# Chunked attention heads of a hybrid encoder layer: score products in two matmuls over stacked high and low halves instead of three

## The chip, the cores and the metric

The kernel runs on one core of one Trainium2 chip. The time is device microseconds (us) of one execution. Engines are named as the profile names them: PE is TensorE's matmul, PEld its weight load, DVE is VectorE, ACT is ScalarE, POOL is GpSimd, SP is SyncE, which here issues the DMAs.

## The reference

One layer: a mixer with eight heads of multi-head latent attention (MLA) and eight heads of chunked attention, then a gated MLP with a causal convolution. 1024 tokens, width 1024. What matters here is the chunked attention:

```python
CHUNK, LEFT_CHUNKS, CA_HEADS, CA_HEAD_DIM = 64, 8, 8, 64
BAND = (LEFT_CHUNKS + 1) * CHUNK

cq = rmsnorm(ca[:, :, 0], g_ca_q[l])
ck = rmsnorm(ca[:, :, 1], g_ca_k[l])
o_ca = chunk_attention(cq, ck, cv, rel_bias[l])

def one_chunk(args):                      # in chunk_attention
    qch, ci = args
    kb = lax.dynamic_slice_in_dim(k_pad, ci * CHUNK, BAND, axis=1)
    vb = lax.dynamic_slice_in_dim(v_pad, ci * CHUNK, BAND, axis=1)
    s = jnp.einsum('bqhd,bkhd->bhqk', qch, kb,
                   preferred_element_type=jnp.float32) * scale + bias[None]
    valid = kj >= (LEFT_CHUNKS - ci) * CHUNK
    s = jnp.where(valid[None, None, None, :], s, NEG_INF)
    p = jax.nn.softmax(s, axis=-1).astype(vb.dtype)
    return jnp.einsum('bhqk,bkhd->bqhd', p, vb)
```

All inputs are float32. The kernel's matmuls take a rounded format (`F32R`), so each float32 operand is split into a high part (the rounded value) and a low part (what is left), and a product is high by high plus high by low plus low by high.

## The kernel before

The attention part interleaves three kinds of work on PE. *Units* are attention: one unit is one head and one group of 512 query tokens, in four tiles of 128 queries. `scores` (line 633) makes a tile's scores, row minima, bias and exponentials, scales and splits the probabilities into 16-bit halves, and has them transposed by DMA; `values` (line 714) multiplies them by the values, three tiles later (`DEPTH`). After four tiles the output page of the unit goes out (lines 724 to 730), through a tile `sb` that ACT writes and DVE adds into a tile `o`, which SP stores. The 16 units of the chunked heads come first, in the order head pair `p`, group `g`, head `o` of the pair; then come 16 MLA units.

*Fillers* are projections: values 0, query-key 1 and 2, values 1, query-key 3, the latents (`f_m`), their up-projections and the output projection of the chunked heads. `pace` (line 810) lets a filler run for a multiple of the cost that `scores` and `values` return. In `gemm3_f` (line 158) each step of a filler is ordered behind the score or value group that stands `LAG` places before the newest one (the list `trail`). A filler of values loads its weights with `load_w` (line 170), whose squares (line 187) use the same two `sq` tiles as the norms of the query-key filler (line 368).

*Pages* are the operands of the scores. For a chunked pair (two heads, 512 tokens) `prep` in `ca_unit` builds a query page and a key page with `qk_page` (line 611): four transposes on PE into one PSUM bank (tag T, one buffer), ACT copies the high half (lines 618, 621), DVE subtracts for the low half (lines 619, 622). Rows 0 to 63 are the first head of the pair, rows 64 to 127 the second; the page's middle index is high or low. The query page has two buffers (tag Q), the key page three (tag K). MLA pages are built by the same function, with 96 rows.

In line 655 a tile's scores are, for each segment of up to 512 keys, query-high by key-high, query-high by key-low and query-low by key-high, over the head's 64 rows. Tiles 0 to 3 of a head have one segment of 128 to 512 keys, tiles 4 to 7 have two with 640 keys together.

The order of instructions on each engine is not written out by hand: the framework draws it from program order, from priorities (the offsets `OFF_S`, `OFF_P`, `OFF_V` pull scores, probabilities and values ahead) and from a simulated timeline. Each engine then works in order.

Of the kernel before, what the change touches and what calls it, by code (L numbers as in the profile page):

```python
# [23 lines left out]
P = 128  # L24
# [38 lines left out]
def layer_kernel(ctx, tc, I, out):  # L63
# [544 lines left out]
                sp.dma_start(part_d[t][:, n * 512:(n + 1) * 512], o[:])  # L608


    def qk_page(src, name, rows, tag, bufs, gain):

        pt = ps.tile([P, 512], F32, name=f"{name}_ps", tag="T", bufs=TB)
        for j in range(4):
            pe.transpose(pt[:rows, j * P:(j + 1) * P], src(j), ident[:])
        pg = at.tile([P, 2, 512], F32R, name=name, tag=tag, bufs=bufs)
        if gain is None:
            act.activation(pg[:rows, 0], pt[:rows], AF.Copy)
            dve.tensor_tensor(pg[:rows, 1], pt[:rows], f32(pg[:rows, 0]), op=SUB)
        else:  # L620
            act.activation(pg[:rows, 0], pt[:rows], AF.Copy, scale=gain)
            dve.scalar_tensor_tensor(pg[:rows, 1], pt[:rows], gain, f32(pg[:rows, 0]), op0=MUL, op1=SUB)
        return pg

    class Unit:

# [6 lines left out]
        def scores(u, i):  # L633

            qpg, kpgs = u.pages()
            bias = u.bias() if u.band else None
            lo = max(0, i - 4) if u.band else 0
            n = (i - lo + 1) * P
            nm = f"{u.nm}_{i}"
            rsum = cst.tile([P, 1], F32, name=f"rs{nm}", tag="rsum", bufs=4)  # L640
            ri = cst.tile([P, 1], F32, name=f"ri{nm}", tag="ri", bufs=4)
            with tc.high_priority(offset=OFF_S):
                s = ps.tile([P, 1024], F32, name=f"s{nm}", tag="S", bufs=2)
                n0 = max(0, min(4, i + 1) - lo) * P
                n1 = n - n0
                c0 = 512 - n0 if n1 else 0
                segs = [(c0, lo * P, n0, 0)] if n0 else []
                if n1:
                    segs.append((512, max(lo, 4) * P - 512, n1, 1))
                q = slice((i % 4) * P, (i % 4 + 1) * P)  # L650
                rs_ = slice(u.base, u.base + u.rows)
                for a in range(2):
                    for c, ko, w, kh in segs:
                        for b in range(2 - a):
                            last = pe.matmul(s[:, c:c + w], qpg[rs_, a, q], kpgs[kh][rs_, b, ko:ko + w],  # L655
                                             start=(a == 0 and b == 0), stop=(a == 1))
# [24 lines left out]
                act.activation(pr[:, :n], sv, AF.Exp, bias=m[:], scale=-1.0, accum_out=rsum[:, 0:1])  # L681
            with tc.high_priority(offset=OFF_P):
                dve.reciprocal(ri[:], rsum[:, 0:1])
                dve.tensor_scalar(ri[:], ri[:], PSCALE, None, op0=MUL)  # L684
                u.pt[i] = []
                for x, (p0, p1) in enumerate(pieces):
                    w = p1 - p0
                    cnt[0] += 1
                    spare = not u.band and cnt[0] % 2
                    if spare:  # L690
                        hl = apg.tile([P, 1024], F16, name=f"hl{nm}_{x}", tag="v16", bufs=6)
                    else:
                        hl = at.tile([P, 1280], F16, name=f"hl{nm}_{x}", tag="HL", bufs=HL_BUFS)
                    pp = pr[:, p0:p1]
                    mode = (MODE_C if u.band else MODE_M)[cnt[0] % 4]
                    if mode == "2":
                        scale_pool(pp, pp, ri[:])
                        act.activation(hl[:, :w], pp, AF.Copy)
                        pool.tensor_tensor(hl[:, w:2 * w], pp, hl[:, :w], op=SUB)
                    else:  # L700
                        if mode == "1":
                            scale_pool(hl[:, :w], pp, ri[:])
                        else:
                            act.activation(hl[:, :w], pp, AF.Copy, scale=ri[:])
                        dve.scalar_tensor_tensor(hl[:, w:2 * w], pp, ri[:], hl[:, :w], op0=MUL, op1=SUB)  # L705
                    if spare:
                        tt = apg.tile([P, 8, P], F16, name=f"PT{nm}_{x}", tag="v16", bufs=6)
                    else:
                        tt = at.tile([P, 10, P], F16, name=f"PT{nm}_{x}", tag="PT", bufs=PT_BUFS)
                    sp.dma_start_transpose(tt[:, :2 * w // P, :], hl[:, :2 * w])  # L710
                    u.pt[i].append((tt, lo + p0 // P, w // P))
            return sum(3 * max(107, w / 2.4) for _, _, w, _ in segs)

        def values(u, i):
            if i % 4 == 0:
                u.pv = ps.tile([P, 512], F32, name=f"pv{u.nm}_{u.g}", tag="pv", bufs=1)
            c = slice((i % 4) * P, (i % 4 + 1) * P)
            todo = [(lo + j, tt[:, h * nk + j, :]) for tt, lo, nk in u.pt[i] for j in range(nk) for h in range(2)]
            with tc.high_priority(offset=OFF_V):
                for x, (j, mov) in enumerate(todo):  # L720
                    last = pe.matmul(u.pv[:, c], u.vst(j), mov, start=(x == 0), stop=(x == len(todo) - 1))  # L721
                trail.append(last.ins)
                if i % 4 == 3:
                    sb = at.tile([P, 512], F32, name=f"sb{u.nm}_{u.g}", tag="sb", bufs=1)
                    dst = at.tile([P, 512], F32, name=f"o{u.nm}_{u.g}", tag="o", bufs=1)
                    r0, r1 = (slice(64, 128), slice(0, 64)) if u.odd else (slice(0, 64), slice(64, 128))
                    inv = vscale[u.vs][1]
                    act.activation(sb[r0], u.pv[r1], AF.Copy, scale=inv[r1])
                    dve.scalar_tensor_tensor(dst[r0], u.pv[r0], inv[r0], sb[r0], op0=MUL, op1=ADD)
                    sp.dma_start(u.dst_d[r0, u.g * 512:(u.g + 1) * 512], dst[r0])  # L730
            return 56 * len(todo)

# [12 lines left out]
    def ca_unit(p, g, o):  # L745
        def prep():
            if g == 0:
                load_bias(2 * p + o)
            if o == 0:
                q = qk_page(lambda j: qns[p, g][:, j, 0:128], f"q{p}_{g}", P, "Q", 2, None)  # L750
                k = qk_page(lambda j: qns[p, g][:, j, 128:256], f"k{p}_{g}", P, "K", 3, gk_ca[:])
                pages["c", p, g] = (q, k)
        u = Unit(f"c{p}{o}", 64 * o, 64,
                 lambda: (pages["c", p, g][0], [pages["c", p, i][1] for i in range(g + 1)]),
                 lambda j: vts[p, j // 4][:, j % 4, o].rearrange("p a b -> p (a b)"),
                 g, True, lambda: biases[2 * p + o], o, oT_d[4 + p], ("c", p // 2))
# [602 lines left out]
```

## Time and profile before

| | |
|---|---|
| runs, median of 3 (lowest to highest) | 1423.73 us (1421.95 to 1424.95) |
| the profiled execution's own time | 1423.74 us |
| its span, first to last instruction | 1422.0 us |
| mean granted PE clock | 0.936 |
| instructions | 19886 |
| chunked-head scores on PE (288 matmuls) | 101.3 to 396.3 us |
| MLA scores on PE (288 matmuls) | 428.4 to 647.3 us |

All profile lines are from one execution. Line numbers (L655) are those of the kernel before. `sc` is the score tile of a chunked head and `sm` that of an MLA head; `Pc`, `hlc`, `PTc`, `pvc` and `oc` are the exponentials, the split probabilities, their transpose, the values' product and the output page of a chunked head. Busy time of PE overlaps from matmul to matmul, as they are pipelined, so the distance of two starts says what one costs.

### The profile page before, as it was taken

To read this page: it belongs to the slowest core of one execution; us is meant where nothing else is said; L and a number is where in the kernel's file an instruction comes from. 1 tells how busy PE (TensorE), PEld (TensorE's weight loads), DVE (VectorE), ACT (ScalarE), POOL (GpSimd) and SP (SyncE) were. 2 spreads that over 40 slices of the span, in tenths; PEclk is the share of its full clock that TensorE was granted. 3 is DMA by queue.
4 is the path that set the end of the run, shared out by engine and by line. 5 is a ranking of instruction groups with operands and counts; after the bars stand their busy time and mean duration, and the time that the engine had idled before them with its cause. 6 is when DMAs were issued, how large, how long until landed. Compare 5 with 4: busy or idle time off the path is not lost.

```text
span 1422.0 us, 19886 instructions
## 1 busy us (share of the span) xinstructions
PE 1247.1 (88%) x6704; PEld 1031.6 (73%) x6704; DVE 1081.8 (76%) x1891; ACT 620.6 (44%) x1150; POOL 686.6 (48%) x673
## 2 busy tenths in 40 slices
PE   3859989998877688886695999999999999999998
PEld 2759977987765567765574887877778777888886
DVE  6864877566689997684467789989888889688667
ACT  4453344334356554453255443343344443543331
POOL 5263545265555673334562675676667775200000
PEclk9979996999888889997896999999999999999999
DMA  8423557545441478778731233333323223894451
GB/s 289 134 74 79 119 111 146 139 107 119 104 94 41 88 163 159 161 148 224 275 126 30 90 111 126 125 122 116 111 84 102 97 96 112 309 356 126 126 163 59
DMA packets 229602, 190.64 MB, mean 134 GB/s; under 512 B 149366, under 2 KB 180218, under 8 KB 228476
## 3 DMA queue, kind: packets, MB, share of 16 engines
q1 hardware_dynamic: 229500, 189.38, 48.1%
q8 instruction: 52, 0.85, 0.2%
q14 instruction: 50, 0.41, 0.1%
HBM read 117.24 MB, written 37.49 MB: 109 GB/s over the span
## 4 chain that ended last, share of the span: by engine, by line
PE 20%; DVE 19%; POOL 5%; issue 5%; ACT 4%; DMA 3%; SPq 1%; DVEq 0%; POOLq 0%; ACTq 0%
DVE u L1024 5%; DVE u L1023 4%; PE dnA_P L1171 2%; PE dnA_P L1173 2%; PE dnA_P L1172 2%; ACT u L1022 2%; PE dnB_P L1173 1%; PE dnB_P L1171 1%; PE dnB_P L1172 1%; DVE gmbc L1010 1%; DVE u L1100 1%; DVE c L1095 1%; DMA adaw<-w_ada 1%; PE p L934 1%; PE p L932 1%
## 5 line engine op out<-in xcount | busy, mean ns | idle before, releaser
L75 ACT ACTIVATE dnP<-dnr 128x1024 fp32r<-128x1024 f32 x73 | 77.4, 1062 | 111.0 <-PE dnA_P L1173 46.4
L1145 DVE TENSOR_TENSOR dnP<-dnr,dnP 128x1024 fp32r<-128x1024 f32 x72 | 88.3, 1230 | 47.0 <-ACT dnP L75 46.4
L1023 DVE SCALAR_TENSOR_TENSOR u<-c,pk,u 128x1023 f32<-128x1023 f32 x44 | 81.8, 1901 | 46.2 <-ACT u L1022 44.8
L71 POOL TENSOR_SCALAR hlm<-Pm,rim 128x512 f16<-128x512 f32 (+3 forms) x96 | 67.2, 710 | 79.6 <-DVE rim L684 36.0
L1024 DVE SCALAR_TENSOR_TENSOR u<-c,pk,u 128x1022 f32<-128x1022 f32 x44 | 84.3, 1955 | 0.0
L71 POOL TENSOR_SCALAR hlc<-Pc,ric 128x640 f16<-128x640 f32 (+2 forms) x64 | 45.3, 710 | 78.8 <-DVE ric L684 31.5
L681 ACT ACTIVATE Pc<-sc,mc 128x640 f32<-128x640 f32 (+2 forms) x64 | 42.1, 659 | 85.9 <-DVE mc L670 64.3
L655 PE MATMUL sm<-mk,mq 96*128 96x512 f32 (+3 forms) x288 | 70.1, 372 | 10.2 <-ACT Pm L681 6.8
L430 DVE SCALAR_TENSOR_TENSOR aacc<-aw,cs,aacc 128x256 f32<-128x256 f32 x84 | 44.5, 529 | 43.1 <-DMA aw<-w_ada 42.4
L655 PE MATMUL sc<-k,q 64*128 64x512 f32 (+3 forms) x288 | 70.6, 374 | 6.4 <-ACT Pc L681 3.8
L721 PE MATMUL pvm<-PTm,vt 128*128 128x128 f16 x576 | 48.2, 235 | 30.0 <-DMA PTm<-hlm 25.7
L705 DVE SCALAR_TENSOR_TENSOR hlm<-Pm,rim,hlm 128x512 f16<-128x512 f32 (+3 forms) x96 | 68.3, 725 | 5.2 <-POOL hlm L71 4.9
L721 PEld LDWEIGHTS <-vt 128*128 128x128 f16 x576 | 39.6, 106 | 40.7 <-issue 38.9
L681 ACT ACTIVATE Pm<-sm,mm 128x128 f32<-128x128 f32 (+3 forms) x64 | 47.2, 737 | 46.6 <-DVE mm L674 23.1
L655 PEld LDWEIGHTS sm<-mk,mq 96*128 96x128 f32 x288 | 49.7, 200 | 19.9 <-ACT Pm L681 10.1
L655 PEld LDWEIGHTS sc<-k,q 64*128 64x128 f32 x288 | 48.1, 209 | 20.3 <-ACT Pc L681 5.2
L1022 ACT ACTIVATE u<-c,pk 128x1024 f32<-128x1024 f32 x44 | 52.2, 1234 | 16.7 <-DVE c L1095 9.3
L75 ACT ACTIVATE wc<-ws 128x512 fp32r<-128x512 f32 x22 | 13.9, 632 | 102.9 <-DVE ws L949 102.9
L150 PE MATMUL ipq<-wq_s,hT 128*128 128x256 f32 x192 | 57.2, 298 | 0.0
L705 DVE SCALAR_TENSOR_TENSOR hlc<-Pc,ric,hlc 128x640 f16<-128x640 f32 (+2 forms) x64 | 48.9, 769 | 9.3 <-POOL hlc L71 9.2
L151 PE MATMUL ipq<-wq_s,hT 128*128 128x256 f32 x192 | 55.8, 291 | 0.0
L152 PE MATMUL ipq<-wq_s,hT 128*128 128x256 f32 x192 | 55.0, 287 | 0.0
(404 smaller groups left out, 4464.9 us busy)
## 6 DMA issues: line engine op xcount, KB each, us to landing
wu<-w_up SPq DMA_DIRECT2D x44, 512.0 KB, 3.5
dnr<-g_d SPq DMA_DIRECT2D x73, 256.0 KB, 4.2
aw<-w_ada SPq DMA_DIRECT2D x96, 128.0 KB, 2.3
g_d<-u SPq DMA_DIRECT2D x22, 512.0 KB, 2.7
dnr<-w_down SPq DMA_DIRECT2D x44, 256.0 KB, 5.4
x<-x SPq DMA_DIRECT2D x16, 512.0 KB, 8.4
adaw<-w_ada_a SPq DMA_DIRECT2D x8, 1024.0 KB, 5.1
g_d<-gs SPq DMA_DIRECT2D x22, 256.0 KB, 2.1
```

What stands on the lines that cost most here:

```text
L71: pool.tensor_scalar(o, i, s, 1.0, op0=MUL, op1=MUL)
L75: act.activation(o, i, AF.Copy)
L150: pe.matmul(pt, sh, mh, start=(start and i == 0), stop=False)
L151: pe.matmul(pt, sh, ml, start=False, stop=False)
L655: last = pe.matmul(s[:, c:c + w], qpg[rs_, a, q], kpgs[kh][rs_, b, ko:ko + w], start=(a == 0 and b == 0), stop=(a == 1))
L681: act.activation(pr[:, :n], sv, AF.Exp, bias=m[:], scale=-1.0, accum_out=rsum[:, 0:1])
L705: dve.scalar_tensor_tensor(hl[:, w:2 * w], pp, ri[:], hl[:, :w], op0=MUL, op1=SUB)
L721: last = pe.matmul(u.pv[:, c], u.vst(j), mov, start=(x == 0), stop=(x == len(todo) - 1))
L1022: act.activation(u[:], c, AF.Identity, scale=pk[:, cv + 2:cv + 3], bias=pk[:, cv + 3:cv + 4])
L1023: dve.scalar_tensor_tensor(u[:, 1:], c[:, :S - 1], pk[:, cv + 1:cv + 2], u[:, 1:], op0=MUL, op1=ADD)
L1024: dve.scalar_tensor_tensor(u[:, 2:], c[:, :S - 2], pk[:, cv:cv + 1], u[:, 2:], op0=MUL, op1=ADD)
L1145: r = f(*a, **k)
```

## The change

The key page of a chunked pair holds, for head `o` of the pair, the high half in that head's own 64 rows and the low half in the other 64 rows; its middle index is now the head. The query high half of each head is a 128-row tile with the same values in both row halves: ACT writes the head's own rows from PSUM, POOL copies them to the other rows. The query low half stays one tile for both heads, each in its own rows. A segment then takes two matmuls: query-high over 128 rows (high by high plus high by low at once), and query-low over the head's 64 rows by key-high. All first matmuls of a tile come before the second ones.

Query pages of MLA become two tiles, high and low, from the same ring as the chunked ones (tag Q2, five tiles of 512 columns, where tag Q had two pages of 1024). `sb` is dropped: ACT writes its part into the output tile, and DVE adds there in place. The costs that `scores` returns to `pace` are unchanged.

```diff
+    def q2(name):
+        return at.tile([P, 512], F32R, name=name, tag="Q2", bufs=5)
+
+    def page_psum(src, name, rows):
         pt = ps.tile([P, 512], F32, name=f"{name}_ps", tag="T", bufs=TB)
         for j in range(4):
             pe.transpose(pt[:rows, j * P:(j + 1) * P], src(j), ident[:])
+        return pt
+
+    def qk_page(src, name, rows, tag, bufs, gain):
+
+        pt = page_psum(src, name, rows)
+        if gain is None:
+            hi, lo = q2(f"{name}h"), q2(f"{name}l")
+            act.activation(hi[:rows], pt[:rows], AF.Copy)
+            dve.tensor_tensor(lo[:rows], pt[:rows], f32(hi[:rows]), op=SUB)
+            return hi, lo
         pg = at.tile([P, 2, 512], F32R, name=name, tag=tag, bufs=bufs)
...
+    def ca_pages(p, g):
+
+        qn = qns[p, g]
+        half = (slice(0, 64), slice(64, 128))
+        pt = page_psum(lambda j: qn[:, j, 0:128], f"q{p}_{g}", P)
+        qh = [q2(f"qh{p}_{g}_{o}") for o in range(2)]
+        ql = q2(f"ql{p}_{g}")
+        for o in range(2):
+            act.activation(qh[o][half[o]], pt[half[o]], AF.Copy)
+            dve.tensor_tensor(ql[half[o]], pt[half[o]], f32(qh[o][half[o]]), op=SUB)
+            pool.tensor_copy(qh[o][half[1 - o]], f32(qh[o][half[o]]))
+        pt = page_psum(lambda j: qn[:, j, 128:256], f"k{p}_{g}", P)
+        kk = at.tile([P, 2, 512], F32R, name=f"k{p}_{g}", tag="K", bufs=3)
+        for o in range(2):
+            act.activation(kk[half[o], o], pt[half[o]], AF.Copy, scale=gk_ca[half[o]])
+            dve.scalar_tensor_tensor(kk[half[1 - o], o], pt[half[o]], gk_ca[half[o]], f32(kk[half[o], o]),
+                                     op0=MUL, op1=SUB)
+        return (qh, ql), kk
...
-                for a in range(2):
-                    for c, ko, w, kh in segs:
-                        for b in range(2 - a):
-                            last = pe.matmul(s[:, c:c + w], qpg[rs_, a, q], kpgs[kh][rs_, b, ko:ko + w],
-                                             start=(a == 0 and b == 0), stop=(a == 1))
+                if u.band:
+                    qh, ql = qpg
+                    for a, rr in ((qh[u.odd], slice(0, P)), (ql, rs_)):
+                        for c, ko, w, kh in segs:
+                            last = pe.matmul(s[:, c:c + w], a[rr, q], kpgs[kh][rr, u.odd, ko:ko + w],
+                                             start=(a is not ql), stop=(a is ql))
+                else:
...
-                    sb = at.tile([P, 512], F32, name=f"sb{u.nm}_{u.g}", tag="sb", bufs=1)
                     dst = at.tile([P, 512], F32, name=f"o{u.nm}_{u.g}", tag="o", bufs=1)
...
-                    act.activation(sb[r0], u.pv[r1], AF.Copy, scale=inv[r1])
-                    dve.scalar_tensor_tensor(dst[r0], u.pv[r0], inv[r0], sb[r0], op0=MUL, op1=ADD)
+                    act.activation(dst[r0], u.pv[r1], AF.Copy, scale=inv[r1])
+                    dve.scalar_tensor_tensor(dst[r0], u.pv[r0], inv[r0], dst[r0], op0=MUL, op1=ADD)
...
-                q = qk_page(lambda j: qns[p, g][:, j, 0:128], f"q{p}_{g}", P, "Q", 2, None)
-                k = qk_page(lambda j: qns[p, g][:, j, 128:256], f"k{p}_{g}", P, "K", 3, gk_ca[:])
-                pages["c", p, g] = (q, k)
+                pages["c", p, g] = ca_pages(p, g)
```

More of the change, by code (lines that the diff above doesn't have):

```diff
@@ L608, in f_oca @@
                 sp.dma_start(part_d[t][:, n * 512:(n + 1) * 512], o[:])
-    def qk_page(src, name, rows, tag, bufs, gain):
+    def q2(name):
+        return at.tile([P, 512], F32R, name=name, tag="Q2", bufs=5)
+    def page_psum(src, name, rows):
         pt = ps.tile([P, 512], F32, name=f"{name}_ps", tag="T", bufs=TB)
@@ L615, in qk_page @@
             pe.transpose(pt[:rows, j * P:(j + 1) * P], src(j), ident[:])
-        pg = at.tile([P, 2, 512], F32R, name=name, tag=tag, bufs=bufs)
[L617 to L622, printed above, removed]
-        return pg
+        return pt
[6 more added lines that the diff above has]
+            return hi, lo
+        pg = at.tile([P, 2, 512], F32R, name=name, tag=tag, bufs=bufs)
+        act.activation(pg[:rows, 0], pt[:rows], AF.Copy, scale=gain)
+        dve.scalar_tensor_tensor(pg[:rows, 1], pt[:rows], gain, f32(pg[:rows, 0]), op0=MUL, op1=SUB)
+        return pg
+    def ca_pages(p, g):
[15 more added lines that the diff above has]
+        return (qh, ql), kk
     class Unit:
@@ L651, in scores @@
                 rs_ = slice(u.base, u.base + u.rows)
-                for a in range(2):
-                    for c, ko, w, kh in segs:
-                        for b in range(2 - a):
-                            last = pe.matmul(s[:, c:c + w], qpg[rs_, a, q], kpgs[kh][rs_, b, ko:ko + w],
-                                             start=(a == 0 and b == 0), stop=(a == 1))
+                if u.band:
[5 more added lines that the diff above has]
+                else:
+                    for a in range(2):
+                        for c, ko, w, kh in segs:
+                            for b in range(2 - a):
+                                last = pe.matmul(s[:, c:c + w], qpg[a][rs_, q], kpgs[kh][rs_, b, ko:ko + w],
+                                                 start=(a == 0 and b == 0), stop=(a == 1))
                 trail.append(last.ins)
```

## The prediction

> **What bounds the kernel now.** I read the page first, for the engines' totals and the granted clock, then stretches of the span, the same stretches for the chunked-head score tiles (`sc`) alone, the order of the matmuls around single score tiles, the query and key pages, and the waits.
>
> ```profile
> PE 1247.1 (88%) x6704; PEld 1031.6 (73%) x6704; DVE 1081.8 (76%) x1891; ACT 620.6 (44%) x1150; POOL 686.6 (48%) x673
> ...
> PEclk9979996999888889997896999999999999999999
> ```
>
> TensorE (PE) leads over the whole span, but an average does not say what one stage waits for. So here are the stretches in which chunked-head scores run, and the multi-head latent stage (MLA) behind them; columns are the stretch, its length, each engine's busy time with its instruction count, clock, DMA share and rate.
>
> ```profile
> 96.00:204.00 108.00, 106.15 (x838) 95.90 (x837) 65.12 (x197) 44.15 (x103) 48.78 (x63) 1.00 0.45 101
> 204.00:222.00 18.00, 13.39 (x73) 10.32 (x73) 15.55 (x44) 11.72 (x36) 11.63 (x13) 0.66 0.60 135
> 222.00:240.00 18.00, 17.15 (x85) 15.08 (x83) 12.37 (x41) 7.01 (x17) 9.57 (x12) 0.50 0.78 152
> 240.00:306.00 66.00, 64.11 (x505) 58.01 (x505) 37.45 (x110) 22.00 (x56) 21.61 (x30) 0.97 0.54 120
> 306.00:400.00 94.00, 82.39 (x506) 69.45 (x506) 61.08 (x180) 40.10 (x128) 55.18 (x106) 0.91 0.56 121
> ...
> 440.00:660.00 220.00, 178.52 (x1226) 146.67 (x1226) 184.14 (x490) 111.01 (x240) 111.27 (x130) 0.92 0.68 132
> ```
>
> From 96 to 204 us PE is busy for 106.15 of 108 us at full clock, from 222 to 306 for 81.3 of 84: there PE is the bound, filled by projections (lines 150 to 152). From 204 to 222 it is not: PE falls to 13.39 of 18. From 306 to 400 PE is busy for 88% and waits for others in between. In the MLA stage VectorE (DVE) is the busiest, 184.14 of 220.
>
> The next rows are the same stretches for `sc` alone (PE, PEld, DVE, ACT).
>
> ```profile
> 96.00:204.00 108.00, 22.76 (x102) 15.01 (x102) 17.87 (x47) 15.99 (x46) 1.00 0.45 101
> 204.00:222.00 18.00, 7.58 (x24) 5.62 (x24) 5.09 (x14) 4.28 (x10) 0.66 0.60 135
> 222.00:240.00 18.00, 6.22 (x18) 4.72 (x18) 4.65 (x12) 3.04 (x7) 0.50 0.78 152
> 240.00:306.00 66.00, 11.25 (x48) 7.07 (x48) 8.77 (x23) 7.95 (x24) 0.97 0.54 120
> 306.00:400.00 94.00, 22.77 (x96) 15.67 (x96) 18.29 (x48) 15.51 (x41) 0.91 0.56 121
> ```
>
> Their matmuls add up to 288: three (high by high, high by low, low by high) for each of 96 segments.
>
> **The matmuls removed.** Two for a segment instead of three: 192 remain, 96 go. A busy time is no price here, as matmuls overlap. The start of a score group and of what follows on PE is one:
>
> ```profile
> 186.67 0.79 PE L655 MATMUL sc<-k,q 64*128 64x384 f32 x3
> 187.38 0.39 PE L150 MATMUL ipq<-wq_s,hT 128*128 128x256 f32 x1
> ...
> 188.05 0.96 PE L655 MATMUL sc<-k,q 64*128 64x512 f32 x3
> 188.94 0.39 PE L151 MATMUL ipq<-wq_s,hT 128*128 128x256 f32 x1
> ...
> 192.86 0.55 PE L655 MATMUL sc<-k,q 64*128 64x128 f32 x3
> 193.34 0.39 PE L150 MATMUL ipq<-wq_s,hT 128*128 128x256 f32 x1
> ...
> 194.25 0.61 PE L655 MATMUL sc<-k,q 64*128 64x256 f32 x3
> 194.79 0.39 PE L150 MATMUL ipq<-wq_s,hT 128*128 128x256 f32 x1
> 195.01 0.28 PE L151 MATMUL ipq<-wq_s,hT 128*128 128x256 f32 x1
> 195.13 0.28 PE L152 MATMUL ipq<-wq_s,hT 128*128 128x256 f32 x1
> ```
> ```profile
> 148.11 1.14 PE L655 MATMUL sc<-k,q 64*128 64x256 f32 x6
> 149.18 0.39 PE L151 MATMUL ipq<-wq_s,hT 128*128 128x256 f32 x1
> ```
>
> Groups of three take 0.48, 0.54, 0.71 and 0.89 us for 128, 256, 384 and 512 keys. Projections of 256 columns follow each other every 0.12 us, so three score matmuls of 256 should take 0.36; the other 0.18 is paid once for each visit to 64 rows and back. It stays, as each score tile still ends with a 64-row matmul. Without it, one matmul is worth (0.48 - 0.18) / 3 = 0.10, then 0.12, 0.18 and 0.24 us. A tile with two segments takes 1.07; a third of (1.07 - 0.18) is 0.30. A head has one tile of each of the first four and four with two segments (640 keys in all): 0.64 + 4 x 0.30 = 1.84 us saved, for eight heads 14.7, or 0.051 us for each of the 288 old matmuls at full clock. A matmul over 128 rows costs no more than one over 64 by these rows (256 wide: 0.12 over 128, the same after the visit's price over 64); the doubled rows are free.
>
> By stretch, with the granted clock: 102 x 0.051 = 5.2; 24 x 0.051 / 0.66 = 1.9; 18 x 0.051 / 0.50 = 1.8; 48 x 0.051 / 0.97 = 2.5; 96 x 0.051 / 0.91 = 5.4. That is 16.8 us gross. The first, third and fourth I count in full (9.5), as PE is the bound there. The second counts nothing: the projections have run out, and the next ones begin at
>
> ```profile
> 222.60 0.56 PE L150 MATMUL ipv<-wv_s,hT 128*128 128x256 f32 x1
> ```
>
> when the second value weights have come through ScalarE (ACT), whose squares go through the `sq` tiles that the norms of the query-key pass use before. That stretch moves earlier whole, by the 5.2 us saved ahead of it. Of the last I take half, 2.7 (bounds 0 and 5.4), since PE also waits for the transposed probabilities there. Realised: 12.2 us.
>
> **The pages.** Each of the eight page pairs (two heads, 512 tokens) has so far
>
> ```profile
> L618 ACT ACTIVATE q<-q_ps x8: 575/582/598, 92.9 to 363.4; 128x512 fp32r<-128x512 f32 x8
> L619 DVE TENSOR_TENSOR q<-q_ps,q x8: 668/684/692, 93.5 to 366.2; 128x512 fp32r<-128x512 f32 x8
> ```
> ```profile
> L621 ACT ACTIVATE k<-k_ps,gk_ca x8: 672/687/697, 98.7 to 368.1; 128x512 fp32r<-128x512 f32 x8
> L622 DVE SCALAR_TENSOR_TENSOR k<-k_ps,gk_ca,k x8: 683/746/751, 99.4 to 368.9; 128x512 fp32r<-128x512 f32 x8
> ```
>
> and each of the four becomes two instructions over 64 rows. Do these cost half? The eviction of an output page has 64 rows and 512 columns on both engines:
>
> ```profile
> L728 ACT ACTIVATE sbc<-pvc,vabc 64x512 f32<-64x512 f32 x15 | 10.2, 683 | 10.2 <-PE pvc L721 10.1
> ```
> ```profile
> L729 DVE SCALAR_TENSOR_TENSOR oc<-pvc,vabc,sbc x16: 672/750/759, 122.6 to 411.8; 64x512 f32<-64x512 f32 x16
> L730 SPq DMA_DIRECT2D oT_d<-oc x16: 452/460/786, 123.4 to 412.6; - x16
> DMA to landing us min/median/max: 2.2/2.5/2.9
> ```
>
> 683 and 750 ns: no less than with 128 rows. So a page pair adds 0.58 + 0.69 = 1.27 us to ACT and 0.68 + 0.75 = 1.43 to DVE; over eight, 10.2 and 11.4. In the five stretches (304 us) DVE is busy for 191.6 and ACT for 125.0, so as work this fits. GpSimd (POOL) gets 16 new copies of 64 x 512. No row has this; the nearest is
>
> ```profile
> L71 POOL TENSOR_SCALAR hlc<-Pc,ric 128x512 f16<-128x512 f32 x8 | 5.5, 692 | 18.1 <-issue 10.0 <-DVE ric L684 5.4 <-DVE ric L683 2.7
> ```
>
> I take 0.69 us, with half and twice as bounds: 11 us (5.5 to 22) beside 146.8 busy of 304.
>
> As latency it is longer. ACT and DVE alternate between the halves, so the PSUM bank of the transposes (one, tag T) comes free one DVE instruction later for q (0.68), and the keys are ready another 0.75 later. Behind it on PE stand the scores, and the projections too: each is ordered behind the score or value group five places back (`LAG`), so PE cannot run far ahead. How often PE stood still for a page is in its waits:
>
> ```profile
> PE pvc L721 <- DMA PTc<-hlc: 8.9, 11, 1.8
> ...
> PE sc L655 <- DVE k L622: 1.9, 2, 1.4
> PE k_ps L615 <- DVE q L619: 1.8, 1, 1.8
> ...
> PE sc L655 <- ACT k L621: 0.8, 1, 0.8
> ```
>
> Four times. The wait for q grows by 0.68, the three for k by 1.43 each: 5.0 us lost. Bounds: 0, if the order found for the changed kernel puts projections there, and 8 x 1.43 = 11.4. I take 5.0 because these waits are the only pages known to have no slack. The copies cost nothing in the sum: the key transposes run beside them; without that cover each page is late by a copy's queue, priced as a rival.
>
> **The rest** I cost at nothing. The query pages become a ring of five half pages; a chunked pair takes three, so its low half waits until the first head of the pair before has been scored. That binds only if pages are built over four tiles ahead, and the waits show pages that come late, not early. Behind such a wait DVE would hold the next row minima. MLA pages take two of the five, with the same instructions. The output eviction loses its second tile: ACT now writes where the last store must have landed, a wait that DVE had before; behind it ACT holds the next exponentials. Sixteen stores from 123.4 to 412.6 us are 19 us apart and land in 2.5, so the tile is free; without that cover it is 2.5 us a time. SP's queue gets no new transfer.
>
> **Sum.** 1423.74 us for the profiled execution (0.01 off the median of the runs, so nothing is converted) - 12.2 + 5.0 = 1416.5 us.
>
> **The rivals.**
> (a) *Larger gain.* All 16.8 us count, no page is late, and the half-clock stretch after the 204 us hole goes: its 17.15 us of PE work at 0.50 would take 8.6, of which 0.9 is already counted, so 7.7 more. 1423.7 - 16.8 - 7.7 = 1399. For it: PE work is dense there. Against: the hole is made by weights, not scores. The Trainium skill ("TensorE: Matmul & The Clock Gate", Part 1) says that about 3.4 us of sustained work brings the full clock back; this trace does not agree, with 0.50 throughout 222 to 240 at 17.15 of 18 us busy. By the rule the 7.7 us would never have been lost.
> (b) *No change.* What PE saves it waits for again at the weights and transposes: 1423.7, give or take 2. For it: 8.9 us of waits for transposes. Against: these fall in the last stretch mostly, and the first has 1.85 us of idle PE in 108.
> (c) *Slower: pages hold PE.* The copies queue on POOL, which works in order and often stands waiting:
>
> ```profile
> POOL hlc L71 <- DVE ric L684: 31.5, 18, 4.3
> ```
>
> 31.5 / 18 = 1.75 us. If every page is late by 1.43 + 1.75 = 3.2 us with nothing in between, 8 x 3.2 = 25.4 less 12.2 gives 1437. It decides from 12.2 / 8 = 1.5 us of PE standing still per page. Against: at least four of the eight pages had slack.
> (d) *Two matmuls don't cost two thirds.* The 128-row and the 64-row part of a tile are different row modes; if the switch between them costs a visit's price on top, 64 tiles x 0.18 = 11.5 us is given back: 1416.5 + 11.5 = 1428. Against: a tile among projections had the way in and the way out before and has the same two now; only score tiles that stand next to each other gain switches. The Trainium skill ("TensorEngine Tiling (Array Packing)", Key Properties) has it that a change of tiling mode drains the engine; the 0.18 us per visit agrees, and by the rule the number of changes matters, not the number of matmuls.
>
> **How the numbers follow.** A measurement of this kernel can tell about 0.2% (2.8 us) from no change. Forecast 0.48, (a) 0.15, (b) 0.12, (c) 0.20, (d) 0.05. Faster (below 1420.9): forecast and (a), 0.63. Same: (b) and part of (d), 0.14. Slower: (c) and the rest of (d), 0.23. The forecast's own range, from all of the last stretch counted and no late page to none of it and all eight late: 1409 to 1426, most of it below 1421. The range over the cases is 1399 to 1432: it leaves out half of (a) and somewhat over half of (c), about 0.2.
>
> **What would show it.** `sc` matmuls 192, groups at 0.38, 0.42, 0.53 and 0.65 us (start to next start) and 0.77 for two segments; (d) shows as 0.18 more. The first projection of the second value weights at about 217 to 219 instead of 222.60. Half-height page instructions at 0.58 to 0.75 us each; if they take half, the 5.0 goes. Waits of PE for pages near 10 us in all; over 17 means (c). The first MLA score 7 us earlier and everything behind it shifted alike; if the later stages change length, the order of instructions there was drawn anew, which I have not priced. A new hole over 8 us of PE before 400, with the clock at 0.50 behind it, would make it wrong, as would POOL copies over 1.4 us.

## The result, and the profile after

| | before | changed |
|---|---|---|
| median (lowest to highest) of 11 runs each | 1426.12 us (1421.95 to 1428.93) | 1434.29 us (1425.77 to 1436.66) |
| the profiled execution | 1423.74 us | 1436.66 us |
| its span | 1422.0 us | 1434.9 us |

The ratio of changed to before is 1.0041, 95% interval 1.0025 to 1.0056: about 6 us slower, where 7.2 us faster was forecast. The changed kernel's profiled execution is its longest run; the comparisons go by the ratios, and single times below are from one execution each. From here on a ratio is always to the kernel before, run beside it on the same chip.

TensorE has less to do and DVE more (line numbers are now those of the changed kernel, where the query page is the tiles `qh` and `ql`, high and low):

```profile
PE 1241.7 (87%) x6608; PEld 1021.4 (71%) x6608; DVE 1107.0 (77%) x1907; ACT 629.7 (44%) x1166; POOL 699.2 (49%) x689
...
PEclk9969987999887889997796999999999999999999
```

The stretches of before in the changed kernel (length, then busy time and instructions of PE, PEld, DVE, ACT, POOL, then clock):

```profile
96.00:204.00 108.00, 98.60 (x730) 89.56 (x731) 65.60 (x181) 43.62 (x100) 50.53 (x65) 0.91 0.44 91
204.00:222.00 18.00, 14.99 (x110) 12.20 (x109) 14.82 (x47) 10.18 (x26) 9.31 (x13) 1.00 0.45 106
222.00:240.00 18.00, 12.98 (x69) 9.76 (x68) 15.95 (x43) 10.81 (x31) 12.72 (x14) 0.53 0.77 166
240.00:306.00 66.00, 64.80 (x517) 58.33 (x518) 45.63 (x129) 27.46 (x67) 28.25 (x39) 1.00 0.58 135
306.00:400.00 94.00, 77.94 (x475) 64.01 (x474) 66.70 (x187) 42.12 (x128) 57.65 (x112) 0.93 0.53 120
...
440.00:660.00 220.00, 180.81 (x1174) 146.41 (x1175) 189.91 (x506) 111.85 (x251) 111.81 (x130) 0.89 0.62 125
```

The first stretch was full of PE work before, 106.15 us of 108 and 838 matmuls; now it holds 98.60 us and 730, at a lower clock. The hole at 204 us has moved to 222.

The score matmuls did fall to 192, and the page instructions of ACT over 64 rows cost what they cost over 128 (0.59 and 0.68 us, before 0.58 and 0.69):

```profile
L683 PE MATMUL sc<-k,qh x96: 220/352/776, 107.3 to 396.4; 128*128 128x128 f32 x24, 128*128 128x256 f32 x24, 128*128 128x384 f32 x24, 128*128 128x512 f32 x24
...
L683 PE MATMUL sc<-k,ql x96: 218/384/793, 107.5 to 396.9; 64*128 64x128 f32 x24, 64*128 64x256 f32 x24, 64*128 64x384 f32 x24, 64*128 64x512 f32 x24
```
```profile
L647 ACT ACTIVATE k<-k_ps,gk_ca 64x512 fp32r<-64x512 f32 x16 | 10.9, 679 | 19.7 <-DVE k L648 10.4 <-PE k_ps L617 9.3
L641 ACT ACTIVATE qh<-q_ps 64x512 fp32r<-64x512 f32 x15 | 8.8, 589 | 12.9 <-DVE ql L642 6.6 <-PE q_ps L617 4.5 <-DVE mc L704 1.7
```

The last two rows (groups by line, from 96 us on, so that one of the sixteen query copies is left out; after the second bar, ACT's idle time ahead of them and who ended it) hold the main finding. ACT stood 10.4 us behind DVE's key instruction and 6.6 us behind DVE's query instruction: ACT's copy of the second head's rows waits for DVE to be done with the first head's. The first page pair of the changed kernel, in order of time, then that of before:

```profile
95.17 0.57 ACT L641 ACTIVATE qh<-q_ps 64x512 fp32r<-64x512 f32 x1
...
96.43 0.67 DVE L642 TENSOR_TENSOR ql<-q_ps,qh 64x512 fp32r<-64x512 f32 x1
97.14 0.59 ACT L641 ACTIVATE qh<-q_ps 64x512 fp32r<-64x512 f32 x1 [0.78 <-DVE ql L642]
97.76 0.69 DVE L642 TENSOR_TENSOR ql<-q_ps,qh 64x512 fp32r<-64x512 f32 x1 [0.21 <-ACT qh L641]
...
103.46 0.68 ACT L647 ACTIVATE k<-k_ps,gk_ca 64x512 fp32r<-64x512 f32 x1 [3.29 <-PE k_ps L617]
104.18 0.75 DVE L648 SCALAR_TENSOR_TENSOR k<-k_ps,gk_ca,k 64x512 fp32r<-64x512 f32 x1 [4.10 <-ACT k L647]
104.96 0.68 ACT L647 ACTIVATE k<-k_ps,gk_ca 64x512 fp32r<-64x512 f32 x1 [0.51 <-DVE k L648]
105.68 0.76 DVE L648 SCALAR_TENSOR_TENSOR k<-k_ps,gk_ca,k 64x512 fp32r<-64x512 f32 x1 [0.38 <-ACT k L647]
```
```profile
92.88 0.57 ACT L618 ACTIVATE q<-q_ps 128x512 fp32r<-128x512 f32 x1
93.49 0.69 DVE L619 TENSOR_TENSOR q<-q_ps,q 128x512 fp32r<-128x512 f32 x1 [0.21 <-ACT q L618]
...
98.71 0.67 ACT L621 ACTIVATE k<-k_ps,gk_ca 128x512 fp32r<-128x512 f32 x1
99.42 0.75 DVE L622 SCALAR_TENSOR_TENSOR k<-k_ps,gk_ca,k 128x512 fp32r<-128x512 f32 x1 [1.69 <-ACT k L621]
```

ACT and DVE do not overlap: four instructions stand in a row, where there were two. The query part takes 98.45 - 95.17 = 3.28 us instead of 1.30, the key part 2.98 instead of 1.46. The built program says the same. In ACT's order of instructions fourteen of the sixteen second halves name DVE as what they wait for, though DVE writes nothing that they read or write. In the query part the two engines share only the PSUM tile that both read, so the framework seems to keep their turns in program order. The first page pair:

```
76 L641 Activation qh_0_0_821<-q_0_ps 64x512 [waits PE_49]
79 L641 Activation qh_0_1_822<-q_0_ps 64x512 [waits DVE_49]
82 L647 Activation k_0_835<-k_0_ps,gk_ca 64x512 [waits PE_49]
84 L647 Activation k_0_835<-k_0_ps,gk_ca 64x512 [waits DVE_49]
```

Each of the three hand-overs also meets whatever the other engine is doing. From the first ACT start to the last DVE end, mean of the eight pages, the query part takes 6.02 us (before 2.45) and the key part 5.09 (3.09): 5.6 us more for a page pair. One page weighs heavily in this mean. The query part of the fifth pair lasts 18.36 us, as its second half stands behind other work of ACT in the hole. Without that pair the query parts are 4.26 and 2.42 us, and a page pair is some 3.8 us longer.

How a longer page becomes time of PE is hard to see in single rows. The longest wait of PE for a transpose, 5.19 us, stands at the third page pair:

```profile
185.29 0.61 PE L617 MATMUL k_ps<-ident,qn 128*128 128x128 f32 x4
185.45 0.48 DVE L430 SCALAR_TENSOR_TENSOR aacc<-aw,cs,aacc 128x256 f32<-128x256 f32 x1 [1.54 <-DMA aw<-w_ada]
...
185.86 1.66 DVE L739 SCALAR_TENSOR_TENSOR hlc<-Pc,ric,hlc 128x640 f16<-128x640 f32 x1
...
187.59 1.35 SPq L744 DMA_TRANSPOSE PTc<-hlc  x1
...
188.74 0.74 DVE L648 SCALAR_TENSOR_TENSOR k<-k_ps,gk_ca,k 64x512 fp32r<-64x512 f32 x1
...
191.08 1.23 PE L755 MATMUL pvc<-PTc,v 128*128 128x128 f16 x10 [5.19 <-DMA PTc<-hlc]
```

The value product stands ahead of the scores in PE's order, so the wait is named after the transposes. The first head's keys were ready at 188.74 + 0.74 = 189.48, before the value product began, and DVE had stood 1.54 us for a DMA ahead of the split (`hlc`) that the transposes wait for. So how much of the 5.19 us is the page's is not shown. PE's own waits for pages are few:

```profile
PE pvc L755 <- DMA PTc<-hlc: 11.8, 9, 5.2
...
PE sc L683 <- DVE k L648: 3.5, 2, 2.0
PE k_ps L617 <- DVE ql L642: 2.7, 2, 2.3
...
PE sc L683 <- POOL qh L643: 1.2, 1, 1.2
```

3.5 + 2.7 + 1.2 = 7.4 us against 4.5 before. The prediction had over 17 us of them as the sign that pages hold PE. Read alone, this list would have called the pages harmless.

### The profile page after: what moved, and what is told of

Its sections match the earlier page's. It is cut to its first block, busy times and chain, and to the rows that moved or that the text cites. A ratio compares the mean times of both kernels' runs of the same rounds, so it can differ in the third digit from the quotient of the medians.

```text
span 1434.9 us, 19790 instructions
## 1 busy us (share of the span) xinstructions
PE 1241.7 (87%) x6608; PEld 1021.4 (71%) x6608; DVE 1107.0 (77%) x1907; ACT 629.7 (44%) x1166; POOL 699.2 (49%) x689
## 4 chain that ended last, share of the span: by engine, by line
DVE 33%; PE 32%; DMA 13%; issue 8%; POOL 7%; ACT 6%; SPq 1%; DVEq 0%; POOLq 0%; ACTq 0%
DMA aw<-w_ada 5%; DVE u L1055 5%; DVE u L1054 4%; PE dnA_P L1202 2%; PE dnA_P L1204 2%; PE dnA_P L1203 2%; PE sc L683 2%; DVE adacc L243 2%; ACT u L1053 2%; DVE hlm L739 2%; PE sm L689 2%; DVE aacc L430 1%; PE dnB_P L1204 1%; PE dnB_P L1202 1%; PE dnB_P L1203 1%
## 5 line engine op out<-in xcount | busy, mean ns | idle before, releaser
L739 DVE SCALAR_TENSOR_TENSOR hlc<-Pc,ric,hlc 128x640 f16<-128x640 f32 (+2 forms) x64 | 53.0, 831 | 5.8 <-POOL hlc L71 5.2
L755 PE MATMUL pvc<-PTc,v 128*128 128x128 f16 x480 | 44.1, 235 | 14.0 <-DMA PTc<-hlc 11.8
L1130 ACT ACTIVATE u<-u 128x1024 f32<-128x1024 f32 x22 | 23.3, 1061 | 71.1 <-DVE u L1055 71.1
L82 POOL TENSOR_TENSOR wc<-ws,wc 128x512 fp32r<-128x512 f32 x22 | 34.6, 1571 | 36.4 <-ACT wc L75 36.4
L1204 PE MATMUL dnA_P<-dnP 128*128 128x512 f32 x132 | 51.4, 389 | 0.0
```

Of the source, the lines that this page charges most:

```text
L1204: pe.matmul(pt, sl, w[:, 0, 0], start=False, stop=stop, skip_group_check=add)
```

## The experiments

Runs with two matmuls on pages that keep the old rows mix two heads in their scores, so they compute something else than the reference and serve for time alone. Only the lines of an edit that matter are shown.

**Matmuls alone.** The kernel before with the new matmuls on its old pages:

```diff
-                        for b in range(2 - a):
-                            last = pe.matmul(s[:, c:c + w], qpg[rs_, a, q], kpgs[kh][rs_, b, ko:ko + w],
+                        for b in range(1 if u.band else 2 - a):
+                            rr = slice(0, P) if u.band and a == 0 else rs_
+                            last = pe.matmul(s[:, c:c + w], qpg[rr, a, q], kpgs[kh][rr, b, ko:ko + w],
```

> The kernel before, pages untouched, with two score matmuls per segment (one over 128 rows, one over 64); the scores then mix two heads and lack high by low. Theory P: before - 12, about 1414. Rival R: before - 4 to before, 1422 to 1426. Rival O: anything from 1412 to 1438, not in the place of the scores.

Measured: 0.9838 (0.9819 to 0.9857), median 1400.29 us, below all three expectations. The same on the changed kernel's ring, with full-height page instructions:

```diff
-        for o in range(2):
-            act.activation(qh[o][half[o]], pt[half[o]], AF.Copy)
-            dve.tensor_tensor(ql[half[o]], pt[half[o]], f32(qh[o][half[o]]), op=SUB)
-            pool.tensor_copy(qh[o][half[1 - o]], f32(qh[o][half[o]]))
+        act.activation(x[:], pt[:], AF.Copy)
+        dve.tensor_tensor(ql[:], pt[:], f32(x[:]), op=SUB)
...
+        act.activation(kk[:, 0], pt[:], AF.Copy, scale=gk_ca[:])
+        dve.scalar_tensor_tensor(kk[:, 1], pt[:], gk_ca[:], f32(kk[:, 0]), op0=MUL, op1=SUB)
```

> Two score matmuls per segment, the changed kernel's ring and in-place output, pages with instructions over 128 rows and no copies (scores mix two heads): the run with two matmuls and old pages, but with the ring. If the removed matmuls are worth 23 us and page instructions take it back (L or C): 1397 to 1405. If the 1400 was luck of one order of instructions (O): 1410 to 1424.

Measured: 0.9919 (0.9903 to 0.9935), 1414.5 us, inside the second expectation (O). The two runs differ by 0.0081 and only in the ring and the output tile, so part of the 1400 was probably the order in which those instructions happened to stand; the second order below bears this out. On the changed kernel's ring the matmuls are worth about 0.8%, 11.6 us.

**Ring and output alone**, in the kernel before:

```diff
+            hi, lo = [at.tile([P, 512], F32R, name=f"{name}{x}", tag="Q2", bufs=5) for x in "hl"]
...
-                    act.activation(sb[r0], u.pv[r1], AF.Copy, scale=inv[r1])
+                    act.activation(dst[r0], u.pv[r1], AF.Copy, scale=inv[r1])
```

> The kernel before with only the ring of five half query pages and the output evicted in place. Theory P: no difference, 1424 to 1428. Rival G (the ring or the shared output tile makes ACT and DVE wait): 5 to 10 us slower, 1431 to 1436. Rival O: a difference of 3 to 10 us of either sign without waits at these tiles.

Measured: 0.9998 (0.9985 to 1.0011). With three matmuls they cost nothing, as forecast.

**A third matmul in the changed kernel:**

```diff
-                    for a, rr in ((qh[u.odd], slice(0, P)), (ql, rs_)):
+                    for x, (a, rr) in enumerate(((qh[u.odd], slice(0, P)), (ql, rs_), (ql, rs_))):
```

> The changed kernel with 288 score matmuls instead of 192: the query-low by key-high product of the chunked heads is added a second time. Theory P (the pages take PE's gain and more, the removed matmuls are worth the 12 us of the prediction): changed + 12, about 1446. Rival R (PE is not what the stage waits for once the pages are late, the matmuls hide): within 4 us of the changed kernel, 1430 to 1438. Rival O (the order of instructions was drawn anew and its luck is the difference): any value between 1420 and 1446.

Measured: 1.0179 (1.0162 to 1.0196), 0.0138 or 19.7 us above the changed kernel, more than the 12 of theory P. PE time does count there; it isn't hidden behind late pages.

**Halves alone**: two matmuls, no copies, old rows, but each page instruction in two.

```diff
+        for o in range(2):
+            act.activation(x[half[o]], pt[half[o]], AF.Copy)
+            dve.tensor_tensor(ql[half[o]], pt[half[o]], f32(x[half[o]]), op=SUB)
...
+            act.activation(kk[half[o], 0], pt[half[o]], AF.Copy, scale=gk_ca[half[o]])
+            dve.scalar_tensor_tensor(kk[half[o], 1], pt[half[o]], gk_ca[half[o]], f32(kk[half[o], 0]),
```

> Two score matmuls per segment; the pages keep the old rows (no copy to the other half, scores mix two heads), but each of the four ACT and DVE page instructions is made in two halves of 64 rows. Theory L (what was lost is the longer chain of ACT and DVE instructions on a page, about 2/3 of it by the run with ACT copies): 15 to 24 us above the run with two matmuls and old pages (1400), so 1415 to 1424. Theory C (it is the copies and what waits for them): within 5 us of 1400. Rival O (luck of the order): neither, and it does not add up with the next run.

Measured: 1.0009 (0.9997 to 1.0021). Against the run with full-height pages (0.9919) that is 0.0090 or 12.8 us, the whole gain of the matmuls. ACT waits for DVE here too, without crossing rows and without copies:

```profile
L640 ACT ACTIVATE qx<-q_ps 64x512 fp32r<-64x512 f32 x16 | 9.4, 587 | 10.6 <-DVE ql L641 6.3 <-PE q_ps L617 4.2
```

**The work of the halves without their chain**: full-height pages, and behind each pair the same number of extra instructions on a tile that no one reads.

```diff
...
+        act.activation(d[half[0]], f32(x[half[0]]), AF.Copy)
+        act.activation(d[half[0]], f32(x[half[1]]), AF.Copy)
+        for o in range(2):
+            dve.tensor_tensor(d[half[1]], f32(x[half[o]]), f32(ql[half[o]]), op=SUB)
```

> The run with two matmuls and full-height pages, plus two ACT and two DVE instructions of 64x512 per page pair behind the page, on a scratch tile that no one reads: the work of the halves without their chain. Chain: 0.990 to 0.995. Work: 0.998 to 1.003, as with the halves.

Measured: 0.9914 (0.9901 to 0.9927), level with 0.9919. In this order the extra work is free, so what the halves cost is the way in which their instructions wait for each other. Which of these waits it is, the run does not say.

**Copies alone**: full-height pages, two POOL copies of 64 rows that the scores read.

```diff
...
+        for o in range(2):
+            pool.tensor_copy(d[half[1 - o]], f32(x[half[o]]))
...
-        return ([x, x], ql), kk
+        return ([d, d], ql), kk
```

> Two score matmuls per segment, page instructions of ACT and DVE over 128 rows as in the kernel before, and two POOL copies of 64 rows per page pair that the scores wait for (scores mix two heads). Theory L: the copies are worth the 11 us by which the run with ACT copies beat the changed kernel, 1408 to 1413. Theory C: 1420 or more. Rival O: below 1403, or more than the changed kernel.

Measured: 0.9999 (0.9982 to 1.0017), median 1422.99 us, as theory C had it, and 0.0080 above full-height pages without copies. With the copies left unread (`[x, x]` again):

> The run with POOL copies alone, but the scores read the original and no instruction waits for the copies. If the copies cost by the wait (chain): back to the run with no copies, ratio to before 0.990 to 0.994. If they cost by POOL's time ahead of the split of the probabilities (work): as with the copies, 0.998 to 1.002.

Measured: 0.9949 (0.9934 to 0.9963), between both expectations. Of the 0.0080, 0.0050 goes when no one waits, and 0.0030 stays with POOL's work and the order that it brings.

**Copies by ACT in the changed kernel**, straight from PSUM:

```diff
-            pool.tensor_copy(qh[o][half[1 - o]], f32(qh[o][half[o]]))
+            act.activation(qh[o][half[1 - o]], pt[half[o]], AF.Copy)
```

> The changed kernel with the 16 copies made by ACT straight from PSUM instead of by POOL. Theory P with the copies' queue on POOL as the main cost: 6 to 10 us faster than the changed kernel, 1424 to 1428. Theory P with the halves on ACT and DVE as the main cost: the same or slower, 1434 to 1440, since ACT gets 9 us of work more. Rival O: either.

Measured: 1.0000 (0.9987 to 1.0012), 0.0041 or 5.8 us below the changed kernel, just short of the first expectation's 6 to 10, and level with the halves alone.

**Pages at a higher priority**, with POOL copies and with ACT copies:

```diff
+                with tc.high_priority(offset=800):
+                    pages["c", p, g] = ca_pages(p, g)
```

> The changed kernel with the chunked pages built at a higher priority (offset 800) than the scores. If the pages' latency is the loss (L), building them earlier wins much of it back: 1410 to 1424. If it is the engines' extra work, nothing: 1430 to 1438.

> ACT copies and the higher priority of the pages together. Theory L: better than either, 1405 to 1418, and so ahead of both kernels. If work and not latency is the loss: 1420 to 1427, as with ACT copies alone.

Measured: 0.9999 (0.9984 to 1.0013) and 1.0019 (1.0004 to 1.0033). With POOL copies it helps by 0.0042, with ACT copies it doesn't. The first lies inside, near the slow edge, of what was expected if latency is the loss, the second in the range for work; so the two do not settle it. The chain itself is as long as in the changed kernel (query part 6.2 us).

**A shorter query chain**, right scores: one ACT and one DVE instruction over 128 rows, then three ACT copies.

```diff
+        act.activation(qh[0][:], pt[:], AF.Copy)
+        dve.tensor_tensor(ql[:], pt[:], f32(qh[0][:]), op=SUB)
+        for o in range(2):
+            act.activation(qh[1][half[o]], f32(qh[0][half[1]]), AF.Copy)
+        act.activation(qh[0][half[1]], f32(qh[0][half[0]]), AF.Copy)
```

> The changed kernel, right scores, with the query high half of both heads taken by one ACT instruction and the low half by one DVE instruction, so that the PSUM bank of the transposes comes free as early as before; three ACT copies of 64 rows then spread the high half to the two tiles. Chain: half of the halves' price comes back against the run with ACT copies (1.000), so 0.994 to 0.997 and ahead of both kernels. Work: 0.999 to 1.002, as ACT has as many instructions.

Measured: 1.0002 (0.9984 to 1.0021), in the range given for work. The query part did become short, 2.30 us from the ACT start to the DVE end, and nothing came back. The copies now stand behind it on ACT, mostly ahead of the keys, and the key part is still in halves; which of the two takes the gain was not separated.

**A second order of the same instructions** (priority offset of the value products 250 instead of 200), for four kernels:

> The kernel before with that offset at 250: a second order of the same instructions. If orders matter little, 1420 to 1428; under O it moves by 5 us or more, to either side.

> The run with two matmuls and old pages (1400), with the priority offset of the value products at 250 instead of 200, which draws a new order on every engine. L or C: 18 to 28 us below the kernel before with the same offset. O: 5 to 15 us below it.

> The run with halves alone in the second order (offset 250). If the halves cost 12 us whatever the order: 1.000 to 1.004 (0.009 above the run with two matmuls in that order, 0.9923). If their price was luck of the first order: 0.990 to 0.996.

> The changed kernel with that offset at 250. L or C: 5 to 15 us above the kernel before with the same offset, and 30 or more above the run with two matmuls and old pages. O: level with or below the kernel before with the same offset.

| | first order | second order |
|---|---|---|
| before | 1 | 1.0041 (1.0021 to 1.0061) |
| two matmuls, full-height pages, old query ring | 0.9838 | 0.9923 (0.9909 to 0.9938) |
| the same on the new ring | 0.9919 | not run |
| and halves | 1.0009 | 1.0038 (1.0025 to 1.0051) |
| and copies: the changed kernel | 1.0041 | 1.0037 (1.0023 to 1.0051) |

The halves cost 0.0090 in the first order on the new ring, and 0.0115 in the second against the old ring; halves and copies together 0.0122 and 0.0114, some 16 to 17 us. Against the old ring in the first order the same differences are 0.0171 and 0.0203. So the pages cost something in both orders, but how much hangs on the order: it alone moved the kernel before by 0.0041, as much as the whole change did, and the two matmuls on the old ring by 0.0085. That the changed kernel is slower than before is not shown beyond the first order; in the second they are level, as the rival O had it. The two matmuls lie 16.8 us below the kernel before there, between the two expectations.

**Pages two tiles sooner in program order**, in the changed kernel with ACT copies and in the kernel before:

```diff
+            v = tiles[n + 2][0] if n + 2 < len(tiles) else u
+            if n == 0 or i % 4 == 0 and not u.band:
...
+            if i % 4 == 2 and v.band:
+                need(v.need)
+                v.prep()
```

> The changed kernel with ACT copies, right scores, and each chunked page pair built two tiles earlier in program order, so that its chain runs beside two tiles of the unit before. If the price is the chain up to the scores: most of the 11.6 us of the removed matmuls shows, ratio to before 0.991 to 0.996, ahead of both kernels. If the chain costs by holding the PSUM bank and PE's order wherever it stands: 0.998 to 1.003.

> The kernel before with its page pairs built two tiles earlier. Control: if only the long pages were late, 0.997 to 1.002; if the old pages were late as well, 0.990 to 0.996.

Measured: 0.9974 (0.9958 to 0.9990), median 1423.16 us beside 1428.01, with right scores: ahead of both kernels by a little, and between the two expectations. The kernel before gets slower by it, 1.0053 (1.0032 to 1.0074), outside both of its own. Under this order of the program the two matmuls with long pages are worth 1.0053 - 0.9974 = 0.0079, about what the matmuls gained with short pages; the order itself gives most of it back.

Over all these orders the kernels with two matmuls fall into two groups. Four with full-height pages and no copies lie at 0.9838 to 0.9923. Ten with instructions in halves, or with copies that the scores read, lie at 0.9974 to 1.0041. Copies that no one reads stand between, at 0.9949. So it does not hang on one order that the pages take the gain of the matmuls back; their exact price does.

## Why the prediction was wrong, point by point

*The matmuls.* The sum came out, -12.2 us forecast and -11.6 measured (0.9919), but that is partly luck. Other pairs that differ in the matmuls alone give 23 us (0.9838), 17 (1.0041 - 0.9923) and 19.7 (the third matmul put back). And in the pair that gives 11.6 the first MLA score stands 428.4 - 412.7 = 15.7 us earlier, of which the MLA stage gave back 6.1. Nor did the parts hold. The distance of starts in the changed kernel:

```profile
204.24 0.22 PE L683 MATMUL sc<-k,qh 128*128 128x128 f32 x1
204.40 0.32 PE L683 MATMUL sc<-k,ql 64*128 64x128 f32 x1
204.65 0.38 PE L150 MATMUL ipq<-wq_s,hT 128*128 128x256 f32 x1
...
206.77 0.28 PE L152 MATMUL ipq<-wq_s,hT 128*128 128x256 f32 x1
206.89 0.28 PE L683 MATMUL sc<-k,qh 128*128 128x256 f32 x1
207.10 0.38 PE L683 MATMUL sc<-k,ql 64*128 64x256 f32 x1
207.41 0.39 PE L150 MATMUL ipq<-wq_s,hT 128*128 128x256 f32 x1
...
208.11 0.34 PE L683 MATMUL sc<-k,qh 128*128 128x384 f32 x1
208.38 0.44 PE L683 MATMUL sc<-k,ql 64*128 64x384 f32 x1
208.75 0.39 PE L152 MATMUL ipq<-wq_s,hT 128*128 128x256 f32 x1
...
211.84 0.39 PE L683 MATMUL sc<-k,qh 128*128 128x512 f32 x1
212.17 0.50 PE L683 MATMUL sc<-k,ql 64*128 64x512 f32 x1
212.60 0.66 PE L617 MATMUL q_ps<-ident,qn 128*128 128x128 f32 x4
```
```profile
154.08 0.46 PE L683 MATMUL sc<-k,qh 128*128 128x256 f32 x2
154.46 0.56 PE L683 MATMUL sc<-k,ql 64*128 64x256 f32 x2
154.95 0.39 PE L152 MATMUL ipq<-wq_s,hT 128*128 128x256 f32 x1
```

Groups take 0.41, 0.52, 0.64 and 0.76 us, not 0.38, 0.42, 0.53 and 0.65, and 0.87 with two segments, not 0.77. A 256-wide matmul is followed after 0.12 us by one of its own height, and after 207.10 - 206.89 = 0.21 by one over 64 rows. So rival (d) was right in part: the switch inside a tile costs some 0.1 us that one way in and out did not have, and a matmul less for each segment saves 0.07, 0.02, 0.07, 0.13 and 0.20 us in these five. For eight heads that is an estimate of 8 x (0.29 + 4 x 0.20) = 8.7 us at full clock, where the prediction had 14.7. The Trainium skill ("TensorEngine Tiling (Array Packing)", Key Properties) has a change of tiling mode drain the engine, and these rows agree. The runs gained more than these rows hold. From the first latent projection (`mp`) to the first MLA value scale (`vspm`) the run with full-height pages needs 79.7 us, the kernel before 94.2:

```profile
306.30:400.50 94.20, 82.59 (x507) 69.65 (x505) 61.50 (x181) 40.24 (x127) 54.88 (x106) 0.91 0.55 120
```
```profile
303.60:383.30 79.70, 70.09 (x419) 59.72 (x417) 53.70 (x150) 36.66 (x117) 50.07 (x104) 0.90 0.55 123
...
412.70:637.70 225.00, 185.59 (x1197) 151.27 (x1197) 190.92 (x515) 115.18 (x257) 110.53 (x133) 0.87 0.63 126
```

while that first `mp` is only 306.3 - 303.6 = 2.7 us earlier, where 9.5 were counted. The two stretches do not hold the same work, though: 48 of 192 score matmuls and 120 value matmuls fall in the shorter one, 96 of 288 and 160 in the longer. So only their sum can be read: `vspm` comes 400.5 - 383.3 = 17.2 us earlier, where 12.2 were forecast. Where the part beyond the matmuls' own rows comes from was not found.

*The pages.* This step failed: 5.0 us forecast for the longer pages, 12.8 measured for the halves alone (0.0090) and 17 with the copies (0.0122). It says that ACT and DVE alternate between the halves, so that each part is longer by one DVE instruction, 0.68 and 0.75 us. They take turns strictly: four instructions and three hand-overs in a row. A page pair became 3.8 us longer from the kernel before to the changed one, the stretched fifth pair left out, and 5.2 from full-height pages to halves alone, the sixth pair's query part left out there, not 1.43. The 12.8 us are above even the upper bound of 11.4, which has all eight pages late by 1.43. Whether the second choice in the step failed as well, that only the four pages for which PE was seen waiting have no slack, the runs do not tell (a fifth such wait, 0.3 us ahead of the query transposes, it had left out): 12.8 us are 1.6 for each of eight pages or 3.2 for each of four. The cause inside the chain, PSUM held too long or scores begun too late, stays open too.

*The copies.* Counted at nothing, since the key transposes run beside them. Alone they cost 0.0080; behind the halves, where the scores are late anyway, 1.0041 - 1.0009 = 0.0032 or 4.6 us in the first order and nothing in the second. With a median of 0.607 us, and one of 1.12, they were no slower than supposed. Rival (c) had the sign and the place, late pages that hold PE, but not the mechanism: it put the price on the copies' queue and kept the 1.43 us.

*The rest.* Ring, output tile and SP's queue cost nothing with three matmuls (0.9998). With two, the new ring stands 0.0081 above the old one in the first order; that this is the order and not the ring is likely, as the old ring came to 0.9923 in the second, but not shown. Extra work on ACT and DVE fits, as said (0.9914).

*The hole.* It came 15 us later (first projection of the second value weights at 237.47 instead of 222.60) instead of 5 earlier. It hardly counted: the first `mp` is at 307.1 against 306.3, as the clock is full soon behind the new hole (1.00 in 240 to 306) and was half for long behind the old one (0.50 in 222 to 240). PE's busy time did not show when it comes back: the kernel before had 0.50 in 228 to 232 at 4.00 us busy of 4, and 0.96 in 240 to 244, behind 3.8 us of projections without a score or value product (from 236.16).

*The later stages.* They were to shift alike. The MLA stage, with the same instructions, took 218.9 us before, 225.0 with full-height pages and 220.2 in the changed kernel. I had named the new order and given it no price; the second order shows it as 0.4% for the kernel before, which is the size of the effect, and as 0.85% for the two matmuls on the old ring.

## What to carry to other kernels

When an instruction that two engines hand to each other through one PSUM tile is split into parts, do not assume that the parts overlap: look in the built order for what the second part waits for, and price the chain with all its hand-overs. In an interleaved kernel the waits that name the page can be a part of its price (here 7.4 us, 2.9 more than before, where the pages cost 17), so compare chain lengths as well. And when the order of instructions is drawn by a program, draw a second one before a difference below one per cent is put down to the change itself.

## What was not expected of the hardware, and what stays open

A matmul over 64 rows behind one over 128 starts about 0.1 us later than behind one of its own height (0.21 against 0.12 us at 256 columns). As the prediction had supposed from the output page, an ACT or DVE instruction over 64 rows and 512 columns takes as long as one over 128: 0.589 and 0.584 us for the query's high half.

Open: which wait in the chain of the halves costs the time, as the shorter query chain gave nothing back. Open as well: whether ACT's two copies placed ahead of DVE's two subtractions, with one hand-over instead of three, would keep the gain; it wasn't tried. Why the higher priority helps the POOL copies and not the ACT copies was not found out either.
